# Moving the second half's preparation later, and refilling two of its products' rows between the last products of the first half

## The chip, the cores and the metric

The kernel runs on one core of a Trainium2 chip. The metric is the device time in microseconds (us) of one execution; lower is better. A profiled execution gives a trace with the start and length of every instruction on TensorE (PE), VectorE (DVE), ScalarE (ACT), GpSimd (POOL) and in the DMA queue of SyncE (SP).

## The reference

One layer of a streaming encoder works on 2048 prompt frames and 32 sample frames of width 1024, in float32:

```
h = rmsnorm(x, ln_g)
q, k, v, gate_a, b_gate, c_gate, u_in, gate_c, merge_a, merge_c = split(h @ w_in)
q, k = rope(rmsnorm(q)), rope(rmsnorm(k))
attn = chunked attention with sinks (q, k, v)
u = c_gate * u_in;  conv = causal 3-tap convolution of u
y_a = (attn * silu(gate_a)) @ w_attn_out
y_c = (b_gate * conv * silu(gate_c)) @ w_conv_out
r = x + (sigmoid(merge_a) * y_a + sigmoid(merge_c) * y_c) @ w_o
out = r + sigmoid(r @ w_ple_gate) * (p @ w_ple_proj)
```

The change lies in the first and largest product, h @ w_in (1024 rows by 42 column tiles of 128), and in what is done beside it.

## The kernel before, in words

**Number format.** Each float32 operand is split into a high and a low part. ACT copies the source to the high part (line 231), DVE subtracts to get the low part (line 232). TensorE then does three matmuls for each product: high by high, high by low, low by high (lines 649, 651, 654).

**Two halves of the tokens.** `HALVES` cuts the tokens in two: the first half with two blocks of 512, the second with two blocks of 528. In each half, h @ w_in is done by a scheme of 2 by 2 blocks that needs seven products in place of eight: x is combined into seven sets of rows (numbered 1 to 7), the weights into seven sums (`make_sums`, lines 357 to 368: four DVE additions for each group), and the results are put together on ACT and DVE when they leave the PSUM banks. The second half uses plain rows for products 1, 6, 7 and 5 and does products 2, 3 and 4 once more by the same scheme, one level down (`run_set`, lines 767 to 817, sets of rows "l", seven small products with the letters A to G).

**The order of the work.** There are G = 21 groups of two column tiles: 0 to 2 make q, k, v ("z"), 3 and 4 the attention gate ("ga"), 5 to 12 alternate between "Cu" and "Bg" (the convolution: a Cu group ends with eight DVE operations of convolution on whole rows, a Bg group with the gating), 13 to 20 are the merge gates ("m"). `steps` (lines 246 to 290) writes the order out. After a start-up, turn i of the loop at line 283 gives products 7 and 5 of group i, product 6 of group i+1, products 3 and 4 of group i, and then products 1 (and 2) of group i+2. In the last turn, i = 20, the two first small products of the second half's product 2 stand in place of product 6. Then follow the rest of the second half's product 2 for all groups ("seconds"), and then the rest.

**What runs beside it.** The loop at line 268 goes through the steps. For each it calls `run` and then, where a table says so:

- `prep` (line 1267): one `next(X1)`. X1 is the generator `second_half` (lines 582 to 601), which prepares x of the second half in fourteen pieces: 1 to 4 compute the RMS factors (square sums on ACT, line 548; transposes on TensorE, a copy to `rb`); 5 to 8 each take four rows of x, normalise them (line 555, four DVE operations), combine them (lines 559 to 562, four DVE operations) and store seven rows to DRAM (`xc`, line 599, by POOL's queue); 9 to 14 are the `quadrants` (lines 615 to 627), which read two rows of `xc`, combine them once more (four DVE operations on half rows) and store four half rows to `xt`. The first product that calls it is product 7 of group 5.
- `refills` (lines 1246 to 1250): after the step named there, `refill(p)` (lines 603 to 610) loads the four rows of product p of the second half from `xc` by SP's queue and splits each into high and low (lines 609 and 610); `refill_set` does the like with seven rows for products 2, 3 and 4. The split rows go to `row` tiles, of which there are 41 (`KP`), or to `xrow` tiles; the loaded rows to the 15 general tiles "t" that the results of the products use as well.

These engines' instructions are not put in the order of the source: in this part of the kernel the framework's scheduler orders each engine's queue by priority (the order of the source) among what its own model of time holds ready. From line 2137 on the order is planned by hand; the change does not touch that part.

Of the kernel before, what the change touches and what calls it, by code (L numbers as in the profile page):

```python
# [42 lines left out]
def tile_hybrid_stream_step(ctx: ExitStack, tc: tile.TileContext, x, xT, pT, wu, consts, rope, ckT, cv_dup,  # L43
# [201 lines left out]
    G = len(groups)  # L245
# [15 lines left out]
    pairs_ = [gs for gs in sets if len(gs) == 2]  # L261
# [10 lines left out]
    for gs in sets:  # L272
        g, e = gs[0], gs[-1]
# [624 lines left out]
    def conv_split(b, cs=range(4)):  # L898
        nt = blk(b)[1]
        for c in cs:  # L900
            yc[b, c] = pair(f"ycs{b}_{c}")
            split_half(yc[b, c][0][:, :nt], yc[b, c][1][:, :nt], conv_in.pop((b, c))[:, :nt])
# [342 lines left out]
    at_step = {x: i for i, todo in enumerate(steps) for x in todo}  # L1245
    refills = {}
    pairs_ = [gs for gs in sets if len(gs) == 2]
    for p, at_ in ((2, (0, G - 1, 2)), (1, (1, pairs_[1], 2, "E")), (6, (1, pairs_[3], 2, "E")), (7, (1, pairs_[5], 2, "E")),
                 (5, (1, pairs_[7], 2, "E")), (3, (1, pairs_[9], 2, "E")), (4, (1, sets[0][1], 6))):
        refills[at_step[at_]] = p  # L1250
    after = {at_step[1, pairs_[9], 2, "C"]: sets[0]}
# [12 lines left out]
    conv_at = {(1, G - 2, 1): lambda: conv_load(0), (1, G - 2, 6): lambda: (conv_split(0), conv_load(1)),  # L1264
               (1, G - 1, 6): lambda: conv_split(1), (1, G - 2, 5): lambda: conv_load(2)}
    conv_at.update({(1, sets[-1], 3 + c % 2, "DE"[c // 2]): lambda c=c: conv_split(2, (c,)) for c in range(4)})
    prep = [at_step[0, g, 7] for g in range(5, G)]
    for i, todo in enumerate(steps):
        if i < NS:
            continue  # L1270
# [956 lines left out]
```

## Time and profile before

| what | us |
|---|---|
| median of three runs | 1521.99 (1521.4 to 1523.32) |
| the profiled execution | 1519.46 |
| its span, first to last instruction | 1517.6 |
| PE busy in the span | 1494.1 |
| DVE busy in the span | 1211.4 |
| ACT busy in the span | 801.1 |

In the rows of the profile an instruction carries the line of the kernel, its engine, its output and inputs by their names, and in brackets how long the engine had been idle before it and who ended that idle time. A view by windows gives the busy time of each engine in a stretch, the granted TensorE clock (PEclk, 1.00 is full speed) and the share of the DMA engines.

### The profile page before, as it was taken

The numbers are of one execution on the slowest core, as the hardware profiler recorded it, in microseconds if no ns is written. First come the engines' busy times: TensorE is split into PE (matmuls) and PEld (weight loads), VectorE is DVE, ScalarE is ACT, GpSimd is POOL, SyncE is SP. The second block draws the span as 40 slices with busy tenths as digits, with TensorE's granted clock in tenths as the row PEclk, the third lists the DMA queues.
The fourth block names the chain that finished last, engine by engine and source line by source line (L and its number), as shares of the span: only waits on it lengthen the run. The fifth ranks groups of instructions, "written<-read, shape, count | busy, mean of one in ns | idle before, by whom it ended". The sixth has DMA issues, their size and how long they took to land.

```text
span 1517.6 us, 28008 instructions
## 1 busy us (share of the span) xinstructions
PE 1494.1 (98%) x9553; PEld 1350.3 (89%) x9553; DVE 1211.4 (80%) x2310; ACT 801.1 (53%) x1908; POOL 399.0 (26%) x582
## 2 busy tenths in 40 slices
PE   9999999989999999999999999999999999999998
PEld 7878777778889999999999999998888888999998
DVE  7896778775568887798976978878899999676777
ACT  8453442334457655443456645687765686442453
POOL 2133233232201253344333321113232202211201
PEclk9999999999999999999999999999999999999999
DMA  9479987787777897643477975678888958989959
GB/s 357 152 273 346 323 301 276 266 280 246 242 235 241 301 318 246 218 144 123 135 252 263 334 244 185 215 246 242 273 214 271 243 172 246 308 253 273 263 168 286
DMA packets 206670, 378.34 MB, mean 249 GB/s; under 512 B 24896, under 2 KB 58496, under 8 KB 206528
## 3 DMA queue, kind: packets, MB, share of 16 engines
q1 hardware_dynamic: 160608, 258.30, 52.3%
q0 software_dynamic: 36272, 100.44, 22.2%
q10 hardware_dynamic: 9648, 17.83, 3.2%
q8 instruction: 75, 1.23, 0.3%
q14 instruction: 67, 0.55, 0.1%
HBM read 246.53 MB, written 130.04 MB: 248 GB/s over the span
## 4 chain that ended last, share of the span: by engine, by line
PE 71%; DVE 3%; DMA 3%; issue 1%; ACT 1%; POOL 0%; SPq 0%; ACTq 0%; DVEq 0%; POOLq 0%
PE b L160 21%; PE yB L160 6%; PE yA L160 6%; PE a L649 5%; PE a L654 5%; PE a L651 5%; PE la L787 4%; PE O L160 2%; PE c L654 2%; PE c L651 2%; PE c L649 2%; PE lc L787 2%; PE S L160 2%; PE pp L160 2%; PE PT L160 1%
## 5 line engine op out<-in xcount | busy, mean ns | idle before, releaser
L160 PE MATMUL b<-xb_h,w 128*128 128x264 f32 (+1 forms) x1344 | 310.8, 323 | 1.3 <-DVE at L160 1.3
L160 PEld LDWEIGHTS b<-xb_h,w 128*128 128x128 f32 x1344 | 222.6, 188 | 19.5 <-DVE at L160 1.8
L649 PE MATMUL a<-x_h,w 128*128 128x264 f32 (+1 forms) x744 | 229.4, 322 | 7.3 <-ACT u L843 6.9
L651 PE MATMUL a<-x_l,w 128*128 128x264 f32 (+1 forms) x744 | 229.6, 322 | 0.0
L160 PE MATMUL b<-xb_l,w 128*128 128x264 f32 (+1 forms) x672 | 216.5, 322 | 0.0
L654 PE MATMUL a<-x_h,w 128*128 128x264 f32 (+1 forms) x744 | 200.5, 322 | 1.8 <-DVE w L232 1.8
L231 ACT CAST w<-wr 128x512 fp32r<-128x512 f32 (+1 forms) x180 | 110.3, 619 | 97.7 <-PE c L654 39.3
L649 PEld LDWEIGHTS a<-x_h,w 128*128 128x128 f32 x744 | 140.6, 189 | 19.7 <-ACT u L843 7.8
L232 DVE TENSOR_TENSOR w<-wr,w 128x512 fp32r<-128x512 f32 (+1 forms) x180 | 132.9, 747 | 29.3 <-ACT w L231 29.1
L651 PEld LDWEIGHTS a<-x_l,w 128*128 128x128 f32 x744 | 140.6, 189 | 10.6
L654 PEld LDWEIGHTS a<-x_h,w 128*128 128x128 f32 x744 | 124.8, 189 | 13.9 <-DVE w L232 3.0
L160 PEld LDWEIGHTS b<-xb_l,w 128*128 128x128 f32 x672 | 126.4, 188 | 8.6
L160 ACT CAST w<-wr 128x512 fp32r<-128x512 f32 x120 | 73.8, 623 | 97.4 <-PE b L160 50.9
L787 PE MATMUL la<-x_h,w 128*128 128x264 f32 x516 | 111.5, 285 | 2.5 <-DVE s2n L803 1.2
L649 PE MATMUL c<-x_h,w 128*128 128x512 f32 (+1 forms) x336 | 110.9, 340 | 0.7 <-ACT x_h L160 0.7
L651 PE MATMUL c<-x_l,w 128*128 128x512 f32 (+1 forms) x336 | 110.8, 339 | 0.0
L654 PE MATMUL c<-x_h,w 128*128 128x512 f32 (+1 forms) x336 | 100.6, 340 | 0.0
L231 ACT CAST w<-a 128x512 fp32r<-128x512 f32 x82 | 49.6, 620 | 93.7 <-DVE a L364 43.6
L160 DVE TENSOR_TENSOR w<-wr,w 128x512 fp32r<-128x512 f32 x120 | 83.8, 704 | 18.8 <-ACT w L160 18.4
L848 DVE SCALAR_TENSOR_TENSOR u<-u,c 128x264 f32<-128x264 f32 (+1 forms) x125 | 59.5, 506 | 49.2 <-ACT u L843 29.0
L160 PE MATMUL yB<-ycs_h,w 128*128 128x264 f32 (+1 forms) x384 | 91.2, 325 | 0.0
L160 PE MATMUL yA<-ac_h,w 128*128 128x264 f32 (+1 forms) x384 | 90.3, 322 | 0.0
(444 smaller groups left out, 3886.7 us busy)
## 6 DMA issues: line engine op xcount, KB each, us to landing
wr<-in_wu SPq DMA_DIRECT2D x161, 256.0 KB, 4.6
a<-in_wu SPq DMA_DIRECT2D x116, 256.0 KB, 4.7
wr<-ws SPq DMA_DIRECT2D x74, 256.0 KB, 4.2
w<-o SPq DMA_DIRECT2D x32, 512.0 KB, 4.9
ws<-a POOLq DMA_DIRECT2D x63, 256.0 KB, 3.9
w<-wa SPq DMA_DIRECT2D x16, 512.0 KB, 5.3
wr<-qs SPq DMA_DIRECT2D x32, 256.0 KB, 4.1
qs<-a POOLq DMA_DIRECT2D x24, 256.0 KB, 5.7
```

The costliest lines, as they stand in the source:

```text
L160: return f(**kw)
L231: nc.scalar.copy(out=hi, in_=src)
L232: nc.vector.tensor_tensor(out=lo, in0=src, in1=hi.bitcast(F32), op=sub)
L649: nc.tensor.matmul(out=ps[:, :cn], lhsT=w[:, 0, k], rhs=x[0][:, c0:c0 + cn], start=first and k == 0, stop=False, skip_group_check=True)
L651: nc.tensor.matmul(out=ps[:, :cn], lhsT=w[:, 0, k], rhs=x[1][:, c0:c0 + cn], start=False, stop=False, skip_group_check=True)
L654: nc.tensor.matmul(out=ps[:, :cn], lhsT=w[:, 1, k], rhs=x[0][:, c0:c0 + cn], start=False, stop=k == 3, skip_group_check=True)
L787: nc.tensor.matmul(out=ps[:, :m], lhsT=w[:, a, k], rhs=r[:, cols], start=q in "ABG" and j == 0 and e == 0, stop=j == 1 and e == 2, skip_gr ...
L848: nc.vector.scalar_tensor_tensor(out=t[:, c0:c0 + cn], in0=t[:, c0:c0 + cn], scalar=-1.0, in1=ps[:, :cn], op0=mul, op1=sub)
```

## The change

The list of refills names other steps for products 1 and 6, and the list of steps after which a piece of X1 is taken is another:

```diff
-    for p, at_ in ((2, (0, G - 1, 2)), (1, (1, pairs_[1], 2, "E")), (6, (1, pairs_[3], 2, "E")), (7, (1, pairs_[5], 2, "E")),
+    for p, at_ in ((2, (0, G - 1, 2)), (1, (0, G - 1, 7)), (6, (0, G - 1, 4)), (7, (1, pairs_[5], 2, "E")),
                  (5, (1, pairs_[7], 2, "E")), (3, (1, pairs_[9], 2, "E")), (4, (1, sets[0][1], 6))):
...
-    prep = [at_step[0, g, 7] for g in range(5, G)]
+    prep = [at_step[0, g, p] for g in range(7, G) for p in ((7, 3) if g >= 15 else (7,))]
```

Product 1's rows of the second half are refilled after product 7 of group 20, the last of the first half, and product 6's rows after its product 4. Both were refilled within the second half's product 2. The pieces of X1 are taken from product 7 of group 7 on instead of group 5, and from group 15 on there are two in a turn, after product 7 and after product 3:

| pieces of X1 | turn before | turn after |
|---|---|---|
| 1 to 4 (RMS factors) | 5, 6, 7, 8 | 7, 8, 9, 10 |
| 5 to 8 (rows of x, eight DVE operations each) | 9, 10, 11, 12 | 11, 12, 13, 14 |
| 9 to 14 (quadrants) | 13 to 18, one each | 15, 16, 17, two each |

No operation is added or dropped.

## Prediction

> **What bounds the kernel now.** I read the page, the waits of PE, PE's timeline around each wait, then the queues of ACT and DVE that ended it, and last the windows group by group.
>
> ```profile
> span 1517.6 us, 28008 instructions
> PE 1494.1 (98%) x9553; PEld 1350.3 (89%) x9553; DVE 1211.4 (80%) x2310; ACT 801.1 (53%) x1908; POOL 399.0 (26%) x582
> ```
>
> PE is busy in all but 1517.6 - 1494.1 = 23.5 us. No matmul is added or dropped, so the change can only alter these gaps and the clock behind them. The waits of PE that it can reach:
>
> ```profile
> PE a L649 <- ACT u L843: 6.9, 2, 4.4
> PE la L787 <- DVE s2n L803: 1.2, 1, 1.2
> PE la L787 <- ACT w L231: 0.7, 1, 0.7
> PE lc L787 <- ACT w L231: 0.6, 2, 0.4
> PE la L787 <- ACT s2n L801: 0.5, 1, 0.5
> ```
>
> The columns are total us, times, longest. The first row is two stalls of the first half; the others lie in the second half's product 2. PE's timeline shows both stalls of the first row:
>
> ```profile
> 266.65 0.50 PE L649 MATMUL a<-x_h,w 128*128 128x512 f32 x1 [2.45 <-ACT u L843]
> 267.68 0.60 PE L651 MATMUL a<-x_l,w 128*128 128x512 f32 x1
> 271.06 0.43 PE L649 MATMUL c<-x_h,w 128*128 128x512 f32 x1
> ...
> 274.13 0.40 PE L651 MATMUL a<-x_l,w 128*128 128x512 f32 x1
> 274.36 0.39 PE L654 MATMUL a<-x_h,w 128*128 128x512 f32 x1
> ...
> 312.53 0.80 PE L649 MATMUL a<-x_h,w 128*128 128x512 f32 x1 [4.44 <-ACT u L843]
> 315.60 0.40 PE L651 MATMUL a<-x_l,w 128*128 128x512 f32 x1
> ```
>
> A stall costs more than its gap. At full speed the matmuls start 0.23 us apart (274.13 to 274.36). Behind the first gap the eight from 267.68 to 271.06 took 3.38 us where 8 x 0.23 = 1.84 would do: 1.5 us more. Behind the second the seven from 312.53 to 315.60 took 3.07 us instead of 1.61: 1.5 us more. So the stalls cost 2.45 + 1.5 = 4.0 us and 4.44 + 1.5 = 5.9 us.
>
> [...]
>
> Why ACT was late:
>
> ```profile
> 264.97 1.14 ACT L231 CAST w<-a 128x512 fp32r<-128x512 f32 x2 [5.69 <-DVE a L364]
> 266.02 0.58 ACT L843 COPY u<-a 128x512 f32<-128x512 f32 x1
> ...
> 310.85 1.14 ACT L231 CAST w<-a 128x512 fp32r<-128x512 f32 x2 [7.69 <-DVE a L364]
> ```
>
> Both times the copy of a PSUM bank (line 843) that PE waits for stands in ACT's queue behind two casts of weights, and those wait for the third weight sum (line 364) of DVE. In DVE's queue that sum stands among the operations of a piece of X1:
>
> ```profile
> 256.56 1.44 DVE L555 SCALAR_TENSOR_TENSOR b<-b,cst,rb 128x528 f32<-128x528 f32 x2
> ...
> 262.35 0.69 DVE L559 TENSOR_TENSOR T<-b,b 128x528 f32<-128x528 f32 x1
> 262.96 0.68 DVE L363 TENSOR_TENSOR a<-a,a 128x512 f32<-128x512 f32 x1
> 263.56 0.70 DVE L560 TENSOR_TENSOR b<-b,b 128x528 f32<-128x528 f32 x1
> 264.19 0.68 DVE L364 TENSOR_TENSOR a<-a,a 128x512 f32<-128x512 f32 x1
> ...
> 278.66 2.14 DVE L555 SCALAR_TENSOR_TENSOR b<-b,cst,rb 128x528 f32<-128x528 f32 x3
> 376.68 0.43 DVE L559 TENSOR_TENSOR xq<-xq,xq 128x264 f32<-128x264 f32 x1
> ```
>
> A rows piece is four normalisations at 2.14 / 3 = 0.71 us and four combinations that come 0.6 us apart when back to back: about 5.3 us of DVE. A quadrants piece is four at 0.43: 1.7 us. Both stalls fall into Bg groups (turns 10 and 12), where the convolution of the Cu group before is still in DVE's queue and a rows piece comes on top. Windows cut at turns 10 to 15, by where product 7's matmuls into bank c begin (columns: length, then busy time and records of PE, PEld, DVE, ACT, POOL, then clock, DMA):
>
> ```profile
> 247.70:271.06 23.36, 20.91 (x83) 16.43 (x82) 19.71 (x32) 6.09 (x11) 6.67 (x13) 0.93 0.77 256
> 271.06:292.72 21.66, 21.66 (x94) 17.49 (x93) 17.93 (x28) 7.04 (x12) 8.00 (x15) 1.00 0.87 295
> 292.72:316.77 24.05, 19.59 (x76) 14.91 (x75) 18.66 (x30) 6.27 (x11) 6.48 (x12) 0.93 0.69 233
> 316.77:336.20 19.43, 19.43 (x85) 15.71 (x84) 14.00 (x23) 9.08 (x16) 5.38 (x10) 1.00 0.84 281
> 336.20:355.70 19.50, 19.50 (x86) 15.81 (x85) 10.84 (x18) 7.98 (x14) 4.31 (x8) 1.00 0.75 237
> ```
>
> A turn has seven products of twelve matmuls, 84 x 0.23 = 19.4 us of PE. The two turns that stalled held the most DVE work (19.71 and 18.66 us); 17.93 us in turn 11 did not stall PE, nor did 14.00 and 10.84 in the merge groups.
>
> **The change part by part.**
>
> Step 1, turn 10 loses its rows piece and gets the fourth RMS piece, whose DVE part is a small copy and a few tiny operations, which I estimate at 1 us from the 0.7 us of a whole row above. Its DVE work goes from 19.71 to about 19.71 - 5.3 + 1 = 15.4 us of 19.4. The third weight sum then comes some 4 us earlier and the 2.45 us stall goes, with its cold tail: -4.0 us. Next late would be the RMS transposes on PE, which come in the middle of a product; that is the same as in turn 8 before. Bounds -4.0 and 0.
>
> Step 2, turn 12 keeps a rows piece (piece 6 for piece 8, with the same eight operations), and turn 11 before it keeps one too (5 for 7). The load of these two turns is the same, so I leave the 5.9 us stall: 0. Bounds -5.9 (it hangs on how the queue happens to interleave) and 0; nearest below is turn 10's, 1.9 us cheaper with the same mix.
>
> Step 3, pieces 7 and 8 go to the merge groups of turns 13 and 14. Turn 13's DVE work becomes 14.00 - 1.7 + 5.3 = 17.6 us, turn 14's 10.84 - 1.7 + 5.3 = 14.4. Both lie below the 17.93 that did not stall. Turn 13 comes near it, so some delay of the weight sums is likely there: +0.5 us. Bounds 0 (there is no idle PE here to win) and +5.9 (a stall like turn 12's) in each. Turns 15 to 17 get a second quadrants piece, +1.7 us of DVE on about 11: 12.7 us of 19.4, hidden by PE; two more loads in SP's queue and four more stores in POOL's per turn, where POOL is busy 4.31 us of 19.50. Turns 5 to 8 only trade light pieces: 0.
>
> Step 4, the refills of 1 and 6. The second half's product 2:
>
> ```profile
> 450.00:461.00 11.00, 11.00 (x60) 9.46 (x60) 7.73 (x16) 6.25 (x12) 0.00 (x0) 1.00 0.48 162
> 461.00:474.00 13.00, 13.00 (x107) 12.87 (x106) 10.76 (x23) 10.31 (x24) 2.16 (x4) 1.00 0.63 213
> 474.00:487.00 13.00, 12.30 (x100) 11.97 (x98) 12.71 (x30) 9.51 (x23) 2.16 (x4) 1.00 0.91 296
> 487.00:502.00 15.00, 14.38 (x113) 13.84 (x112) 14.20 (x34) 9.78 (x23) 4.88 (x5) 1.00 0.77 258
> ...
> 461.24 1.85 SPq L609 DMA_DIRECT2D xr<-xc  x4
> 473.69 2.19 SPq L609 DMA_DIRECT2D xr<-xc  x4
> ...
> L231 ACT CAST x_h<-xr x37: 617/634/665, 433.3 to 544.9; 128x528 fp32r<-128x528 f32 x37
> L232 DVE TENSOR_TENSOR x_l<-xr,x_h x37: 696/700/710, 434.4 to 548.5; 128x528 fp32r<-128x528 f32 x37
> ```
>
> From 474 to 502 DVE is busy 26.9 of 28 us: here it is the bound, and PE idles 0.70 + 0.62 us. Each refill is four casts of 0.63 us on ACT and four subtractions of 0.70 us on DVE. Refill 1 (loads at 461.24) moves to about 447, into turn 20, and refill 6 (loads at 473.69) about to where refill 1 was. So 2.8 us of DVE leave the full stretch and 2.8 us enter 450 to 461, where DVE has 11.00 - 7.73 = 3.3 us free and ACT 4.75. The rows have room: of 41, product 7 and 5 of the first half hold 8 + 4 and refill 2 holds 14, which leaves 15 for the 8 of refill 1; after product 7, eight more come free for refill 6. The three stalls in the full stretch that wait for ACT's weights, the 0.7 and 0.6 us of the waits, should go: -1.3 us. The other two belong to refills 5 and 3, which stay. Bounds -3.1 (all four rows) and +1.8 (below).
>
> What can make it cost time is a wait at the head of ACT's queue:
>
> ```profile
> 438.01 0.63 ACT L231 CAST x_h<-xr 128x528 fp32r<-128x528 f32 x1 [1.13 <-DMA xr<-xt]
> 478.76 1.28 ACT L231 CAST x_h<-xr 128x528 fp32r<-128x528 f32 x2 [1.45 <-DMA xr<-xc]
> 502.14 0.64 ACT L231 CAST x_h<-xr 128x528 fp32r<-128x528 f32 x1 [3.32 <-DMA xr<-xc]
> ```
>
> The cast waits for its load, and behind it wait casts of weights and copies of PSUM banks, and PE for these. Refill 5's 3.32 us stand just ahead of the 1.2 us stall. The nearest row for a refill between first-half products is refill 2's at 438.01: 1.13 us, and no stall of PE. So I take 0, and 1.2 + 0.5 = 1.8 us (what the two worst refills cost) as the bound.
>
> Sum: -4.0 + 0 + 0.5 - 1.3 = -4.8 us. What PE gains here lasts, since PE is the bound through to the end and the part planned by hand has no fixed times. The profiled execution took 1519.46 us, 1.9 more than its span, and would take 1514.7. The median of the runs before, 1521.99, is 2.5 above it; shifted by the same -4.8 it becomes 1517.2 us.
>
> **The rivals.**
>
> Turn 12's stall goes as well. For it: turn 10's was shorter with the same mix, so the stall is no fixed price, and turns 9 and 10 leave DVE no backlog now. Against: turns 11 and 12 hold exactly the old load. Time: -4.8 - 5.9 = -10.7, 1511.3 us.
>
> The stall only moves. Turn 13's DVE comes to 17.6 us, within 0.4 of a load that did not stall but also within 1.1 of one that did (18.66). If it stalls like turn 10, -4.0 and +0.5 become nothing: -1.3 us, 1520.7. The same comes out if the scheduler, whose order shifts with every change, opens another gap of that size.
>
> Slower. Pieces 7 and 8 hold up the weight sums in turns 13 and 14 as piece 8 did in turn 12, since by priority they go ahead of the sums, and ACT's queue stops behind them: two stalls of 5.9 us, less 4.0 and 1.3: +6.5 us, 1528.5. It decides from the point where a turn's sums come later than its PSUM copies can wait, on this profile between 17.93 and 18.66 us of DVE work in a turn. Turn 14 with 14.4 speaks against it.
>
> The refills do not really move, because their loads wait for free "t" tiles, which the results of turn 20 hold: then step 4 is 0 and the total -3.5 us, 1518.5, within the forecast's own range.
>
> **How the numbers follow.** Forecast (total between -2 and -8): 0.50. Turn 12 goes too: 0.15. The stall moves: 0.21. Slower: 0.14. A measurement of this kernel can tell about 0.2%, 3.0 us, from no change. Of the forecast's 0.50 some 0.41 lies beyond -3.0; with 0.15 that is 0.56 faster. Same is 0.09 + 0.21 - 0.02 = 0.28, where 0.02 is for a moved stall that is worse than the old one; slower 0.14 + 0.02 = 0.16. The range takes in turn 12's case and the moved stall with the +1.8 us of the refills and some noise of the scheduler, -11.5 to +2.0: 1510.5 to 1524.0 us; outside are the slower case and the tails. The likeliest case alone spans 1514 to 1520.
>
> **What would show it.** Step 1: no gap of PE at L649 behind ACT's L843 in turn 10, and PEclk 1.00 there. Step 2: one such gap of 2 to 5 us in turn 12. Step 3: DVE work of about 17.6 us in turn 13, PE full. Step 4: loads of line 609 near 447 and 456, DVE below 95% from 474 to 487, the waits for ACT's L231 gone. The prediction is wrong if the gap of turn 10 is still there with no rows piece in it, if new gaps stand in turns 13 to 20, or if PE's gaps sum to more than 23.5 us.

## The result, and the profile after

| | before | after |
|---|---|---|
| median, us (beside each other on one chip) | 1522.28 (1521.4 to 1523.32, 4 runs) | 1503.67 (1503.57 to 1504.2, 4 runs) |
| the profiled execution, us | 1519.46 | 1504.2 |
| its span, us | 1517.6 | 1502.4 |
| PE busy in it, us | 1494.1 | 1488.8 |

The ratio is 0.9878, with a 95% interval of 0.9861 to 0.9895: 18.6 us faster, 13.5 us below the forecast of 1517.2 and below the low end of its range, 1510.5. The sign was forecast, the size was not.

The head of the page after:

```profile
span 1502.4 us, 27997 instructions
PE 1488.8 (99%) x9553; PEld 1349.2 (90%) x9553; DVE 1211.5 (81%) x2310; ACT 801.8 (53%) x1908; POOL 399.1 (27%) x582
```

The work is the same on every engine. PE's gaps have gone from 23.5 us to 1502.4 - 1488.8 = 13.6, and PE's busy time is 5.3 us shorter: two stretches of 3.41 us at a clock of 0.50 are gone (last section), and with the waits the slow starts right behind them, as where two matmuls came 0.34 us apart at a clock of 1.00 (216.44 to 216.78 in before).

The waits of PE, after (total us, times, longest), those in reach of the change:

```profile
PE la L787 <- ACT w L231: 1.9, 3, 1.4
...
PE lc L787 <- DVE w L232: 0.4, 1, 0.4
...
PE a L649 <- ACT w L231: 0.2, 1, 0.2
```

No row names ACT's line 843 any more: both stalls, 6.9 us in the row of before, have gone. One window, 180 to 430 us of the first half, shows it best. First before, then after (columns as in the prediction's windows):

```profile
180.00:430.00 250.00, 241.67 (x1022) 192.50 (x1021) 181.31 (x295) 92.93 (x175) 71.32 (x132) 0.99 0.79 266
```

```profile
180.00:430.00 250.00, 250.00 (x1083) 202.17 (x1082) 187.56 (x308) 109.22 (x212) 71.92 (x132) 1.00 0.84 289
```

In the same 250 us PE gets through 1083 matmuls in place of 1022, and has no idle time left. 61 matmuls at 0.23 us are 14.0 us, so this stretch holds nearly the whole gain of the profiled execution (15.2 us of span).

Where in the stretch? The starts of TensorE's weight loads, counted from the first one, can be set side by side in two traces (a few records are missing, so a difference is good to about 0.5 us). By this count the kernel after is ahead of before by 3.45 us in turn 9 (at 240 of before), by 8.19 behind turn 10's stall, by 8.80 ahead of turn 12's, by 14.89 behind it, and by 14.84 in turn 18. Product 2 of the second half adds about 0.7.

Turns 10 to 14 in the trace after, cut every 19.5 us, since no turn stalls:

```profile
242.00:261.50 19.50, 19.50 (x87) 15.72 (x86) 16.05 (x26) 6.81 (x14) 3.65 (x7) 1.00 0.51 160
261.50:281.00 19.50, 19.50 (x86) 15.81 (x85) 16.14 (x25) 5.78 (x11) 7.22 (x14) 1.00 0.89 315
281.00:300.50 19.50, 19.50 (x85) 15.77 (x85) 17.95 (x30) 6.48 (x11) 6.36 (x13) 1.00 0.73 254
300.50:320.00 19.50, 19.50 (x85) 15.74 (x85) 17.72 (x28) 8.06 (x14) 7.15 (x14) 1.00 0.95 325
320.00:339.50 19.50, 19.50 (x86) 15.75 (x85) 14.20 (x23) 8.76 (x16) 5.96 (x12) 1.00 1.00 358
```

The fourth column, DVE's work, is close to what the prediction worked out: 16.05 us for 15.4 in turn 10, 17.72 for 17.6 in turn 13, 14.20 for 14.4 in turn 14. Turn 12 holds 17.95 us, about what it held before (18.66 in a window of 24.05), and PE does not stall in it.

What has changed in turn 12 stands in ACT's queue:

```profile
294.77 0.58 ACT L843 COPY u<-a 128x512 f32<-128x512 f32 x1
298.74 0.62 ACT L231 CAST w<-a 128x512 fp32r<-128x512 f32 x1 [3.39 <-DVE a L364]
```

ACT still waits 3.39 us for the third weight sum, but it waited 7.69 before, and the copy of the PSUM bank now stands ahead of the cast that waits. Before, the copy stood behind it (311.90 behind the cast at 310.85). DVE is no faster. From the operation that starts the turn's convolution work to the third sum, in before and then in after:

```profile
295.72 0.69 DVE L848 SCALAR_TENSOR_TENSOR u<-u,c 128x512 f32<-128x512 f32 x1 [3.55 <-PE c L654]
...
310.08 0.68 DVE L364 TENSOR_TENSOR a<-a,a 128x512 f32<-128x512 f32 x1
```

```profile
282.39 0.69 DVE L848 SCALAR_TENSOR_TENSOR u<-u,c 128x512 f32<-128x512 f32 x1 [1.42 <-PE c L654]
...
297.95 0.68 DVE L364 TENSOR_TENSOR a<-a,a 128x512 f32<-128x512 f32 x1
```

That is 14.4 us before and 15.6 us after. But this chain begins earlier beside PE: its first operation, which waits for PE to fill bank c, comes 13.3 us earlier (295.72 to 282.39) where PE as a whole is 8.8 us ahead. In before, PE runs products 3 and 4 of group 11 behind product 7 of group 12, in after ahead of it. So the third sum, 12.1 us earlier, comes 3.3 us earlier beside PE. No engine works faster; two orders have changed, PE's and ACT's. What the copy's place alone costs was measured in group 5 below: about 1.2 of the 4.44 us. The rest hung on the sum, and on the cast that waits for it.

The loads of the two refills:

```profile
433.13 1.92 SPq L609 DMA_DIRECT2D xr<-xc  x4
446.57 1.99 SPq L609 DMA_DIRECT2D xr<-xc  x4
```

With the 15 us that the kernel is ahead, these are 448 and 461 on the clock of before: the refills did move, refill 6 into the place of refill 1.

### The profile page after: what moved, and what is told of

It is laid out like the page before. It is cut to its first block, busy times and chain, and to the rows that moved or that the text cites. A ratio compares the mean times of both kernels' runs of the same rounds, so it can differ in the third digit from the quotient of the medians.

```text
span 1502.4 us, 27997 instructions
## 1 busy us (share of the span) xinstructions
PE 1488.8 (99%) x9553; PEld 1349.2 (90%) x9553; DVE 1211.5 (81%) x2310; ACT 801.8 (53%) x1908; POOL 399.1 (27%) x582
## 4 chain that ended last, share of the span: by engine, by line
PE 89%; DMA 5%; DVE 3%; issue 1%; ACT 1%; SPq 0%; POOL 0%; DVEq 0%; ACTq 0%; POOLq 0%
PE b L160 21%; PE a L654 7%; PE a L649 7%; PE a L651 7%; PE yB L160 6%; PE yA L160 6%; PE la L787 5%; PE c L654 3%; PE c L651 3%; PE c L649 3%; PE pp L160 3%; PE lc L787 2%; PE O L160 2%; PE S L160 2%; DMA xr<-xc 2%; PE PT L160 1%
```

## The experiments

All but those of the fourth group start from the kernel before. In the expectations A is the theory that nearly the whole gain comes from the place of X1's pieces, C that delays add up over turns in a row until PE stalls, and D that a Bg turn with a rows piece stalls by itself. The table gathers the leads over before, worked out from the weight loads as above; the marks are times of before.

| kernel | rows pieces in turns | lead at 240 | at 273 (turn 10) | at 321 (turn 12) | ratio to before |
|---|---|---|---|---|---|
| after | 11, 12, 13, 14 | 3.45 | 8.19 | 14.89 | 0.9878 [0.9861, 0.9895] |
| prep_only | 11, 12, 13, 14 | 3.50 | 8.23 | 14.94 | 0.9893 [0.9877, 0.991] |
| refills_only | 9, 10, 11, 12 | 0.18 | 1.73 | 0.70 | 0.9977 [0.9967, 0.9986] |
| rms_late | 9, 10, 11, 12 | -1.61 | 2.69 | 3.60 | 0.9967 [0.9955, 0.9979] |
| rows_late | 11, 12, 13, 14 | 0.44 | 4.82 | 11.52 | 0.9902 [0.9887, 0.9916] |
| rows_apart | 9, 10, 13, 14 | -0.36 | -0.37 | 6.33 | 0.9952 [0.993, 0.9975] |
| one_later | 10, 11, 12, 13 | 3.53 | 7.88 | 8.85 | 0.9941 [0.9918, 0.9963] |
| bg_rows | 10, 12, 13, 14 | 0.21 | 4.57 | 11.24 | 0.9901 [0.9871, 0.993] |
| cu_rows | 9, 11, 13, 14 | 0.24 | 4.52 | 11.21 | 0.9913 [0.9879, 0.9947] |
| cast_pool | 9, 10, 11, 12 | 0.04 | 2.85 | 2.35 | 0.9971 [0.9961, 0.9981] |
| cast_dve | 9, 10, 11, 12 | 0.01 | 2.66 | 3.20 | 0.9962 [0.9947, 0.9976] |

### 1. The two parts alone

prep_only has the new `prep` and the old refills:

```diff
-    prep = [at_step[0, g, 7] for g in range(5, G)]
+    prep = [at_step[0, g, p] for g in range(7, G) for p in ((7, 3) if g >= 15 else (7,))]
```

> The pieces of X1 as in the changed kernel, refills 1 and 6 where they were before. Theory A (the whole gain comes from where the pieces of X1 stand): 1503 to 1506 us, 16 to 19 below the kernel before, no wait of PE for ACT's L843 in turns 10 and 12. Rival R (the earlier refills give a fair part, at least 3 us): 1507 us or more. By the prediction's own step 4 (1.3 us) it would be 1505.

Measured: 1505.22 us median. refills_only has the old `prep` and the new list of refills:

```diff
-    for p, at_ in ((2, (0, G - 1, 2)), (1, (1, pairs_[1], 2, "E")), (6, (1, pairs_[3], 2, "E")), (7, (1, pairs_[5], 2, "E")),
+    for p, at_ in ((2, (0, G - 1, 2)), (1, (0, G - 1, 7)), (6, (0, G - 1, 4)), (7, (1, pairs_[5], 2, "E")),
```

> The pieces of X1 as before, refills 1 and 6 moved. Theory A: within 1.5 us of the kernel before (1521 to 1524), with both stalls of 2.45 and 4.44 us still there. Rival R: 1519 or less, and fewer waits between 470 and 520 us.

Measured: 1517.75 us median. Its trace keeps both stalls:

```profile
PE a L649 <- ACT u L843: 6.9, 2, 4.5
```

Product 2 of the second half, 430 to 530 us, in before, refills_only, prep_only and after:

```profile
430.00:530.00 100.00, 96.85 (x667) 89.73 (x665) 81.14 (x168) 66.07 (x143) 15.38 (x24) 1.00 0.77 262
```

```profile
430.00:530.00 100.00, 98.34 (x689) 92.05 (x688) 81.49 (x169) 67.76 (x147) 18.85 (x27) 1.00 0.81 273
```

```profile
430.00:530.00 100.00, 97.00 (x726) 92.81 (x725) 79.78 (x169) 66.42 (x149) 22.98 (x35) 1.00 0.80 270
```

```profile
430.00:530.00 100.00, 97.63 (x730) 93.32 (x729) 81.18 (x172) 66.96 (x149) 24.67 (x36) 1.00 0.79 271
```

PE's idle time there is 3.15, 1.66, 3.00 and 2.37 us, though a kernel that is ahead has more of product 2 in this window. By the weight loads product 2 gains 2.4 us in refills_only, 0.2 in prep_only and 0.7 in after. So the pieces give 16.3 us of the 18.6; the refills give 3.8 by themselves, and on top of the pieces 1.5, which the two intervals do not tell from none. A holds for prep_only. Its forecast for refills_only, within 1.5 us of before, fell, and the rival's, 1519 or less, came true. The leads of refills_only at turns 10 and 12 are no work of the refills: the gaps are those of before (2.45 and 4.47 us), and what differs is the clock behind them (last section).

### 2. Which pieces

In rms_late the four RMS pieces are squeezed into turns 7 and 8 and the rows pieces stay; in rows_late the RMS pieces stay in turns 5 to 8 and the rows pieces go to turns 11 to 14, as in the kernel after:

```diff
-    prep = [at_step[0, g, 7] for g in range(5, G)]
+    prep = [at_step[0, g, p] for g in range(7, G) for p in ((7, 3) if g <= 8 else (7,))]     # rms_late
+    prep = [at_step[0, g, p] for g in range(5, G) if g not in (9, 10) for p in ((7, 3) if g >= 15 else (7,))]     # rows_late
```

> Only the four RMS pieces are later: two each in turns 7 and 8; the rows pieces stay in turns 9 to 12, the refills as before. Theory A (the rows pieces on top of the convolution make the two stalls, the light pieces the small delays of turns 5 to 9): both stalls remain, 1518 to 1521. Rival L (the light pieces start a backlog that reaches the stalls): the stalls shrink to under half, 1512 to 1516.

Measured: 1516.21 us. Turn 10's stall went, but turn 12's stayed at 3.8 us, and two RMS pieces in one turn made gaps of their own, 1.34 us at 215.5 us (the other of the two in the first row) and 2.31 us at 226.4 (lead -1.61 us). Neither theory had this. PE's waits from 180 to 330 us:

```profile
PE a L649 <- ACT u L843: 5.2, 2, 3.8
PE rps L532 <- DVE dg L530: 2.9, 2, 2.3
```

> The RMS pieces stay in turns 5 to 8, the rows pieces move from turns 9 to 12 to turns 11 to 14, the quadrants go two a turn from 15 on; refills as before. Theory A: both stalls gone though turns 11 and 12 still have a rows piece each, 1507 to 1511. Rival L: the stall of turn 12 remains, 1513 to 1518.

Measured: 1506.49 us, with no stall in turn 10 or 12. Where the rows pieces stand decides turn 12's stall; turn 10's hangs on the RMS pieces as well, since rms_late lost it with its rows pieces in place. What rows_late lacks against prep_only is the lead from turns 5 to 9, where the RMS pieces still stand: 3.1 us in the profiled executions (3.50 - 0.44), 1.3 us in the medians, where the two intervals overlap.

### 3. How many in a row, and in which turns

Four kernels differ only in the turns that they leave out (first column of the table for the rest):

```diff
+    prep = [at_step[0, g, p] for g in range(5, G) if g not in (11, 12) for p in ((7, 3) if g >= 15 else (7,))]     # rows_apart
+    prep = [at_step[0, g, p] for g in range(6, G) for p in ((7, 3) if g >= 15 else (7,))]     # one_later
+    prep = [at_step[0, g, p] for g in range(5, G) if g not in (9, 11) for p in ((7, 3) if g >= 15 else (7,))]     # bg_rows
+    prep = [at_step[0, g, p] for g in range(5, G) if g not in (10, 12) for p in ((7, 3) if g >= 15 else (7,))]     # cu_rows
```

> RMS pieces in turns 5 to 8 and refills as before; rows pieces in turns 9, 10, 13 and 14. Theory C (delays add up: turn 10 stalls because turns 5 to 9 leave VectorE no slack, turn 12 because of turns 9 and 10 before it): turn 10 keeps its gap of 2 to 3 us, turn 12 has none, 1514 to 1517. Rival D (a rows piece in a Bg turn stalls by itself unless the scheduler happens to interleave well): turn 10 stalls, 1514 to 1517 as well, but see the two next runs.

> All pieces one turn later: RMS in turns 6 to 9, rows in turns 10 to 13, the quadrants from turn 14 on, refills as before. Theory C: turn 10 has only its first rows piece, so its gap is gone or under 1 us; turn 12 is the third in a row and stalls by 1 to 4 us: 1507 to 1513. Rival D: both Bg turns hold a rows piece and stall, 1515 to 1520.

> Rows pieces in turns 10 and 12 (the two Bg turns that stalled), 13 and 14; RMS pieces and refills as before. Theory C: with turns 9 and 11 free of them, neither Bg turn stalls by over 1 us: 1505 to 1510. Rival D: both stall, 1516 to 1520.

> Rows pieces in turns 9 and 11 (Cu turns), 13 and 14; RMS pieces and refills as before. Theory C: no stall over 1 us in turns 9 to 12, 1505 to 1510, like the run with rows in 10 and 12. Rival D: no stall either, 1505 to 1510; then only the run with rows in the Bg turns tells the two apart.

Measured: 1513.1, 1511.13, 1506.15 and 1508.04 us. In rows_apart turn 10 stalls and turn 12 does not; in one_later it is the other way round; in bg_rows and cu_rows neither does. The rows of PE's waits, rows_apart and then one_later (the other two have no such row):

```profile
PE a L649 <- ACT u L843: 2.5, 1, 2.5
```

```profile
PE a L649 <- ACT u L843: 3.8, 1, 3.8
```

The time of rows_apart lies 0.9 us below what both theories gave; the other three lie where C had them. D falls: in bg_rows both Bg turns, 10 and 12, hold a rows piece and neither stalls. The pattern is that of C. Where the RMS pieces stand in turns 5 to 8, turn 10 stalls with rows pieces in both 9 and 10, and with one of the two it does not. Turn 12 stalls with rows pieces in 10, 11 and 12 (before, refills_only, rms_late, one_later) and in no kernel that leaves one of them out.

ACT's queue in one_later shows both cases in one trace. In turn 10 the copy is ahead of the waiting cast, in turn 12 behind it:

```profile
255.78 0.58 ACT L843 COPY u<-a 128x512 f32<-128x512 f32 x1
260.03 0.62 ACT L231 CAST w<-a 128x512 fp32r<-128x512 f32 x1 [3.67 <-DVE a L364]
...
301.96 1.14 ACT L231 CAST w<-a 128x512 fp32r<-128x512 f32 x2 [7.03 <-DVE a L364]
303.00 0.58 ACT L843 COPY u<-a 128x512 f32<-128x512 f32 x1
```

The wait of 3.67 us costs PE nothing, that of 7.03 costs 3.77. All seven stalls of turn 10 or 12 in the kernels so far have this second form, and PE's gap is ACT's wait less 3.2 to 3.3 us each time: 5.69 and 2.45, 7.69 and 4.44, 7.03 and 3.77. So the length of the wait counts beside the copy's place: the waits of 3.4 to 3.7 us with the copy ahead are also the short ones.

### 4. The refills of 7, 5 and 3

These start from the kernel after, once more run beside them, and move three more refills:

```diff
-(7, (1, pairs_[5], 2, "E")), (5, (1, pairs_[7], 2, "E")), (3, (1, pairs_[9], 2, "E"))
+(7, (1, pairs_[3], 2, "E")), (5, (1, pairs_[5], 2, "E")), (3, (1, pairs_[7], 2, "E"))     # one_set_earlier
+(7, (1, pairs_[1], 2, "E")), (5, (1, pairs_[3], 2, "E")), (3, (1, pairs_[6], 2, "E"))     # all_earlier
+(7, (1, pairs_[7], 2, "E")), (5, (1, pairs_[9], 2, "E")), (3, (1, sets[2], 2, "F"))     # one_set_later
```

> The kernel after, once more, beside the two that follow, so that all three are compared on one chip: 0.988 of the kernel before (1502 to 1506 us).

> The kernel after, with the refills of products 7, 5 and 3 in the second half's second product one set of outputs earlier. Theory (what is left is the order in which blocks of x's rows are refilled; the second product still idles about 2.4 us in the profile after): 1 to 2 us less than the kernel after. Rival (the gaps of the second product are set by ScalarE's and VectorE's evictions of that product, not by the refills' places): within 1 us of the kernel after, gaps moved. Second rival (an earlier refill waits for the readers of the block it overwrites, and SyncE's queue holds up what is behind): 1 to 3 us more.

> The same three refills, two to three sets earlier than in the kernel after. Theory: 1 to 2.4 us less than the kernel after, and no less than with one set. Rival (evictions set the gaps): within 1 us. Second rival (the earlier refill waits for readers): 2 to 5 us more, more than with one set.

> The kernel after, with the refills of products 7, 5 and 3 two sets later in the second half's second product (7 and 5 one place on in the list, 3 behind the single set). Moving them earlier cost 3 to 6 us, so the place of a refill has a price here. Theory (a refill is dear because its casts wait at the head of ScalarE's queue for their loads in a stretch where VectorE has no slack, and fewer of them in that stretch is better): about 1 to 2 us less than the kernel after (0.987 of the kernel before). Rival (the list of the kernel after is at its best place, and any move opens gaps): 2 to 6 us more (0.990 to 0.993).

Measured: 1503.41 (after_again), 1509.11, 1506.68 and 1502.66 us; ratios to before 0.988 [0.9865, 0.9895], 0.9922 [0.9908, 0.9937], 0.9896 [0.988, 0.9913] and 0.9881 [0.9864, 0.9897]. Earlier is worse: by 5.7 us in one_set_earlier, whose interval lies above that of after_again, and by 3.3 us in all_earlier, whose interval overlaps it. So no gain came, as the second rival said, but it had 1 to 3 us for one_set_earlier, and the larger move as the dearer one. The profiled execution of one_set_earlier, 1512.38 us, is the slowest of its four, so its waits may be longer than usual. Between 430 and 540 us, one_set_earlier against after, the waits of ACT for the loads of rows grow and PE's waits for ACT's weights with them:

```profile
PE la L787 <- ACT w L231: 3.6, 3, 1.6
PE lc L787 <- ACT w L231: 2.4, 3, 1.3
```

```profile
ACT x_h L231 <- DMA xr<-xc: 16.5, 12, 3.4
```

The kernel after has 1.9 us in 3 for the first of PE's rows and none for the second, and for ACT's:

```profile
ACT x_h L231 <- DMA xr<-xc: 11.5, 6, 3.7
```

This fits the prediction's worry, a cast at the head of ACT's queue that waits for its load; no run takes that wait away by itself. Later is no better than after by what was measured: PE idles only 1.00 us from 430 to 530 in one_set_later, but the intervals of the two ratios are the same. No version was found that beats the kernel after beyond doubt.

### 5. The waiting cast taken out of ACT's queue

Is the copy's place behind the waiting cast the cause, or is DVE late with the weights in any case? Two kernels leave all pieces and refills at their old places and give the two casts (product 6 of groups 12 and 14) to another engine:

```diff
-    def split(hi, lo, src):
-        nc.scalar.copy(out=hi, in_=src)
+    def split(hi, lo, src, copy=nc.scalar.copy):
+        copy(out=hi, in_=src)
...
-            split(w[:, 0, :n], w[:, 1, :n], raw_of.pop(i)[:, :n])
+            split(w[:, 0, :n], w[:, 1, :n], raw_of.pop(i)[:, :n], nc.gpsimd.tensor_copy if worder[i] in (("s", 0, 12, 6), ("s", 0, 14, 6)) else nc.scalar.copy)
```

> The kernel before, with X1's pieces and the refills at their old places; two casts of weights (product 6 of groups 12 and 14, whose sum is the third one of turns 10 and 12) are made by GpSimd in place of ScalarE, so that the copy of the PSUM bank no longer stands behind a cast that waits for that sum. DVE's work and its order up to the two sums are the same. Queue theory (the stall is the copy's place in ScalarE's queue, behind the waiting cast): no PE gap behind the copy of line 843 in turns 10 and 12, TensorE 4.3 and 6.1 us earlier behind them, 1507 to 1513 us (0.991 to 0.995). Load theory (VectorE is late with the weights themselves, and PE would wait for them in any case): the gaps stay within 1 us, now behind the weights (lines 231 or 232), 1518 to 1522 us.

Measured: 1515.97 us, between the two forecasts. PE's waits from 180 to 430 us:

```profile
PE a L649 <- ACT u L843: 3.6, 3, 1.2
PE c L649 <- DVE u L848: 1.8, 1, 1.8
```

The gaps of 2.45 and 4.44 us became 1.19 us each, though the sums were as late as before. A third gap behind the copy, 1.18 us in turn 11, is new, and one of 1.81 us in turn 12 opens behind DVE's line 848. GpSimd was slow with the casts (2.09 and 1.55 us), but DVE's waits from 255 to 320 us were for PE, loads and ACT, none for GpSimd. cast_dve is the same with `nc.vector.tensor_copy`; up to the second half's product 2 it leaves PE's order as it was.

> As cast_pool, but VectorE makes the two casts itself, right behind the sums, so that no other engine's queue stands still for them: VectorE gets 2 x 0.7 us more work in the turns that stall, ScalarE 2 x 0.6 us less, and up to the second half TensorE's order stays as it was. Queue theory: TensorE's two gaps shrink to the 1.2 us that cast_pool showed, with no cold tail, and no new gap comes with them: about 2.8 us less behind turn 10 and 4 to 5 us less behind turn 12, 1510 to 1515 us, less than cast_pool. Load theory (VectorE's work in the turn is what stalls TensorE): with 0.7 us more of it both gaps stay or grow, 1520 to 1524 us.

Measured: 1514.71 us, ratio 0.9962 [0.9947, 0.9976].

```profile
PE a L649 <- ACT u L843: 2.4, 2, 1.2
PE c L649 <- DVE u L848: 2.2, 1, 2.2
```

ACT's queue in turn 10 shows why 1.19 us stay:

```profile
264.20 0.62 ACT L231 CAST w<-a 128x512 fp32r<-128x512 f32 x1 [4.95 <-PE c L654]
264.72 0.58 ACT L843 COPY u<-a 128x512 f32<-128x512 f32 x1
```

Of the two casts ahead of the copy only one was moved. The other is still there, and it waits for PE's product into bank c, the one just ahead of the product that needs the copy; in turn 12 it is the same (4.96 us), and in cast_pool in turns 10 to 12 (4.95, 4.88 and 4.96 us). So 1.18 to 1.19 us is what the copy's place behind a cast costs when the third sum is out of the way. Turn 10 came out as the queue theory has it: 2.66 us ahead of before, nothing lost after. Turn 12 did not. The gap behind the copy shrank to 1.19 us, but twelve matmuls on a new gap of 2.25 us opens behind DVE's line 848, which reads bank c and stands in DVE's queue behind the piece and the sums; with its cold tail (eight matmuls in the 3.40 us from 312.22 to 315.62) it leaves a gain of 0.5 us. The load theory's forecast, both gaps the same or longer, fell in turn 10 and half held in turn 12: there DVE is late by itself, and the copy's place was only the first of two ways in which PE met that (the 1.81 us of cast_pool stand at the same place).

## Why the prediction was right or wrong

**Step 1 (turn 10): the size right, the reason only in part.** -4.0 forecast. The lead grew by 4.3 us across turn 10 in every kernel that lost this stall by leaving a rows piece out of turn 9 or 10 (8.19 - 3.45 = 4.7 in the kernel after, of which 0.4 stands ahead of the stall). The chain that the prediction read, copy behind cast behind third sum, is the one that cast_dve confirms, for 2.66 us of it. But the reason given, that turn 10 loses its own rows piece, is not the condition: bg_rows keeps a rows piece in turn 10, rms_late in both 9 and 10, and neither stalls there.

**Step 2 (turn 12): this is the step that failed.** "The load of these two turns is the same, so I leave the 5.9 us stall: 0." The load was the same (17.95 us) and the stall went: 6.1 us, about its lower bound of -5.9. The reason given was the wrong measure. A turn's own DVE work does not decide; the runs show that it takes rows pieces in turns 10, 11 and 12 together. In the trace, the third sum came 3.3 us earlier beside PE, ACT's wait for it fell from 7.69 to 3.39 us, and the copy stood ahead of it. In the kernel after, turns 9 and 10 are free of rows pieces, as the rival "turn 12's stall goes as well" said, and the counter-argument that outweighed it was the one about the load. The prediction's own windows held the hint: 17.93 us did not stall and 18.66 did, a difference of one operation, too thin to be a limit. (Its windows are cut at product 4 of the group before, not at product 7: DVE's line 709, which follows product 4 of a Cu group, comes right behind the matmuls that begin at 292.72. The comparison of like stretches does not change by that.)

**Step 3: right in turns 13 to 17, wrong in turns 5 to 8.** Turn 13 got 17.72 us of DVE and lost nothing (+0.5 forecast). But "turns 5 to 8 only trade light pieces: 0" left out 3.45 us: PE had waits and slow matmuls there before, and with the RMS pieces two turns later they are gone. In the medians less of it is seen, the 1.3 us between rows_late and prep_only. The largest wait, in before:

```profile
216.44 0.50 PE L654 MATMUL a<-x_h,w 128*128 128x512 f32 x1 [1.08 <-DVE w L232]
```

The kernel one_later, with the RMS pieces one turn later, gains the same 3.53 us; rows_late, with them in place, 0.44. The pieces are light for DVE, but they came where it had no slack: in before DVE is busy 6.95 of the 7.00 us from 210 to 217.

**Step 4: within its bounds, but not by its reason.** -1.3 forecast. In the profiled execution product 2 gained some 0.7 us, in the medians prep_only and after are 1.5 apart. The waits for ACT's weights did not go, though (1.9 us in 3 after; 0.7 and 0.6 before); the wait for DVE's line 803 did. Nor did DVE get slack: where below 95% was the sign, it is busy 13.00 of 13.00 us at the same place in after (459.7 to 472.7).

**The sum.** As measured in the two traces the parts are 3.5 us up to turn 9, 4.7 in turn 10, 0.6 between turns 10 and 12 (four slow matmuls at 296 to 297 us in before), 6.1 in turn 12 and 0.7 in product 2: 15.6 us, which agrees with the 15.3 between the two profiled executions as far as the count of weight loads goes. Of it 10.2 us, turn 12 with the matmuls ahead of it and the turns up to 9, had been put at nothing. The other 3.3 us of the 18.6 lie between a profiled execution and the median. The prediction shifted the median by the sum, but before's profiled execution was 2 to 4 us faster than the four runs beside it, and after's the slowest of four by 0.4 us. A part of this is likely the cold tails, which differ from one execution to the next (below): the mean granted clock of before's profiled execution was 0.998, that of most other executions of before on record 0.995 to 0.997. How many us that makes was not measured.

**What stays open.** The framework's scheduler makes these orders from its own model of time, and the traces show the orders, not its reasons. In before, PE runs product 3 of groups 9 to 12 behind product 7 of the next group; in the kernel after those of 9 to 11 are back in the order of the source. That fits a delay that is carried from turn to turn, but one_later has it in groups 6 to 13 (in group 9 by one matmul only) and stalls once, so it is not enough by itself. That three rows pieces in a row are needed is what six placements of them show, not a rule that was derived. No kernel was run that changes the copy's place alone, with both casts left on ACT.

## What to carry to other kernels

A stall that hangs on what stands ahead in an engine's queue, as in before the copy at 266.02 stood behind casts that had waited 5.69 us, is not priced by the work of its own stage: ask what the stages before it hand on, and look in the waiting engine's queue for what stands behind the waiting instruction and whether it could stand ahead of it. Where steps of side work are handed out one in a turn, a turn or two without them, or a later start, can be worth more than their own time; it is cheap to try which turns. And before a stage is put at nothing because it only trades light work, look whether PE is full there.

## What the runs showed of the hardware

The cold tail, the slow matmuls behind a gap, is not fixed. The stretch behind the 2.45 us gap of turn 10, and that behind the gap of turn 12, in refills_only and in before:

```profile
266.40:271.10 4.70, 4.60 (x20) 3.75 (x21) 4.00 (x8) 1.77 (x4) 1.07 (x2) 1.00 0.98 325
312.00:316.00 4.00, 4.00 (x11) 3.13 (x10) 1.42 (x3) 1.10 (x2) 0.04 (x1) 0.50 0.97 323
```

```profile
266.60:271.30 4.70, 4.65 (x13) 3.69 (x14) 2.60 (x6) 1.11 (x3) 1.07 (x2) 0.64 0.99 320
312.50:316.50 4.00, 3.97 (x11) 3.23 (x12) 2.60 (x5) 1.10 (x2) 1.21 (x3) 0.63 0.96 315
```

The same gap of 2.45 us was followed by a clock of 1.00 in one execution (refills_only, 20 matmuls) and by one of 0.64 in the other (before, 13 matmuls), and the tail behind the gap of 4.4 us differs too. In before the half clock starts at 267.71 and at 312.08 and holds 3.41 us each time; from 264.00 to 267.71, from 271.12 to 274.50, from 308.66 to 312.08 and from 315.49 to 319.00 the clock is 1.00:

```profile
267.71:271.12 3.41, 3.41 (x10) 2.64 (x9) 1.48 (x3) 1.10 (x2) 0.33 (x1) 0.50 0.98 302
312.08:315.49 3.41, 2.96 (x7) 2.41 (x8) 2.66 (x5) 1.40 (x3) 1.63 (x4) 0.50 0.93 323
```

Behind turn 12's gap the slow matmuls, 0.42 to 0.43 us from one start to the next, run from 311.44 to 315.71 in refills_only, 4.27 us, and from 313.12 to 315.25 in before, 2.13 us. Why the clock dropped behind the gap of 2.45 us in one execution and not in the other was not shown. The prediction took the slow matmuls of one execution as part of that gap's price, and they are one outcome of two. In one_set_earlier the clock was 0.66 behind two gaps, of 0.57 us (ended at 495.44) and 1.61 us (ended at 497.81):

```profile
497.80:502.00 4.20, 4.19 (x24) 4.19 (x25) 3.48 (x7) 2.04 (x6) 0.29 (x1) 0.66 0.76 222
```

A cast of 128x512 from float32 took 0.62 us on ACT (before), 0.42 and 0.47 us on DVE (cast_dve), and 2.09 and 1.55 us on GpSimd (cast_pool).
